# A quarter of a depthwise convolution's taps: from VectorE to ScalarE, summed by adding transfers

## The chip, the cores and the metric

The kernel runs on one core of a Trainium2 chip. Time is the device time of one execution in microseconds. The engines of a core work side by side, each through its own list of instructions in order: TensorE (PE, matrix products), VectorE (DVE), ScalarE (ACT), GpSimd (POOL) and SyncE (SP, which here only starts transfers). An instruction can wait on semaphores that other engines or transfers raise; everything behind it on its engine waits with it. A transfer is started by an instruction of SP, ACT or POOL and runs by itself afterwards.

## The reference

A two-layer trunk over 256 latent tokens and 256 context tokens of width 1024. In each layer one input projection feeds a convolution branch and an attention branch. The part that matters here is the convolution branch:

```python
def conv_branch(p_glu, dw, dw_b, ln_g, ln_b, w_o):
    a, g = jnp.split(p_glu, 2, axis=-1)
    u = a * jax.nn.sigmoid(g)
    u = dwconv1d(u, dw, dw_b)                 # depthwise, 31 taps, 512 channels
    u = jax.nn.silu(layernorm(u, ln_g, ln_b))
    return u @ w_o
```

Each of 512 channels is convolved with its own 31 weights. With channels on partitions that is 4 groups of 128 channels (j = 0 to 3) and 31 taps (t) each: 124 products of a shifted 128x256 tile with one weight per channel, summed by group. The second layer computes its output for the latent tokens alone.

## The kernel before

All matrices are float32. A product is made of three matrix products of rounded parts (L197 to L199): weight high part by input high part, weight high part by input low part, weight low part by input high part. So each unit of weights (128x1024, 512 KB) is loaded by SP into one of four `raw` buffers, rounded by ACT to `whi` (L167), and the rest `wlo` is taken by DVE (L168). For some units, listed in `ADDED`, the low part is made otherwise (`wadded`): ACT writes minus the high part into `wlo` (L217), and a transfer that POOL starts adds `raw` to it (L218). In the second layer these are three units: the query of head pair 1, the query of head pair 2, and gate 2.

The second layer's work on PE goes in this order: GLU groups 0, 1 and 2 (each gives one tile `u` of the convolution's input), the four V units in two halves (L736; ACT copies the first half's sums at L724, the second half's at L721), query 0 and key 0, GLU group 3, gate 0, query 1, key 1, and so on with attention between, then gates, the two branch products, the output product and the feed-forward part. After the first V half is copied, SP starts 16 small transfers that gather windows of V (`VW`, L728); the next weight loads stand behind these in SP's list.

The convolution is `tap` (L665 to L673): tap 0 writes `cb[j]` with the bias, each later tap is one DVE instruction that multiplies and adds into `cb[j]`. The taps of a group are put in a list when its `u` is written (L693). A generator takes three of them at each slot between matrix products; `layer_norm` takes the rest and then sums the four `cb` tiles, on POOL for the first two sums (L949, L950). `conv_tap` holds a tap back until the newest score operation of attention has been issued.

The program is written in one sequence; a scheduling layer then sorts each engine's instructions by its own estimate of when each can run, keeps the data dependences by semaphores, and gives out the buffers of a rotating pool in that order. So the place of an instruction in an engine's list is not read off the source.

Of the kernel before, what the change touches and what calls it, by code (L numbers as in the profile page):

```python
# [8 lines left out]
F32 = mybir.dt.float32  # L9
F32R = mybir.dt.float32r  # L10
BF16 = mybir.dt.bfloat16
AF = mybir.ActivationFunctionType
ALU = mybir.AluOpType
AX = mybir.AxisListType

P = 128
# [3 lines left out]
S = 256  # L20
# [5 lines left out]
TAPS = 31  # L26
# [15 lines left out]
BADA, N1G, DW, DWB, LNG, LNB, N2G, FDW, FDB, NPAR = 0, 48, 56, 180, 184, 188, 192, 200, 332, 376  # L42
# [11 lines left out]
def trunk(ctx: ExitStack, tc: tile.TileContext, xt, cvec, crow, wall, wada, params, bias_t, rope_t, out):  # L54
    nc = tc.nc
    pe, act, dve, pool, sp = nc.tensor, nc.scalar, nc.vector, nc.gpsimd, nc.sync
# [11 lines left out]
    def nm(s):  # L68
        uid[0] += 1
        return f"{s}_{uid[0]}"  # L70
# [3 lines left out]
    def psum(tag="main"):  # L74
        return psp.tile([P, 512], F32, tag=tag, bufs=BANKS[tag], name=nm(tag))

    def tmp(w=512):
        return tp.tile([P, w], F32, tag="t", bufs=5, name=nm("t"))
# [39 lines left out]
    par = cp.tile([P, DEPTH * NPAR + KD], F32, name="par")  # L118
# [27 lines left out]
    def pr(l, off, n):  # L146
        return par[:, l * NPAR + off : l * NPAR + off + n]
# [211 lines left out]
    def sum_squares(n, T, apart=False):  # L359

        at = tp.tile([P, 512], F32, tag="ss", name=nm("ss"))
        return [SumSq(T, at[:, i * T : (i + 1) * T], apart) for i in range(n)]
# [246 lines left out]
    for k in range(KD):  # L609
        if k % 2 == 0:  # L610
            sp.dma_start(x2[k // 2].rearrange("p i t -> p (i t)"), xt[k // 2])
        q = tp.tile([P, 512], F32, tag="ss", name=nm("ss")) if k == KD - 2 else tmp()
# [19 lines left out]
    for l in range(DEPTH):  # L632
        last = l == DEPTH - 1
# [4 lines left out]
        with ExitStack() if last else start as e1a:  # L638
            ea = e1a.enter_context(tc.tile_pool(name=f"ea{l}", bufs=1)) if last else ea0
# [4 lines left out]
            NU_ = KC  # L644
            us = [ea.tile([P, NS, S + 2 * PAD], F32, name=f"u{l}_{i}") for i in range(NU_)]
# [12 lines left out]
            after = [None]  # L658

            def conv_tap(j, t):  # L660
                if after[0] is not None:
                    with tc.issue_after(after[0].ins):
                        tap(j, t)
                else:
                    tap(j, t)  # L665

            def tap(j, t):
                w = par[:, l * NPAR + DW + j * TAPS + t : l * NPAR + DW + j * TAPS + t + 1]
                src = us[j % NU_][:, :, t : t + S]
                if t == 0:  # L670
                    dve.tensor_scalar(cb[j], src, w, pr(l, DWB + j, 1), ALU.mult, ALU.add)
                else:
                    dve.scalar_tensor_tensor(cb[j], src, w, cb[j], ALU.mult, ALU.add)  # L673

            rate = [0.0]

# [248 lines left out]
            with ExitStack() as e1c:  # L925
# [12 lines left out]
                def layer_norm():  # L938

                    while taps:  # L940
                        for _ in range(6 if last else 5):
                            if taps:
                                conv_tap(*taps.pop(0))
                        yield
                    pace[0] = 1.0 if last else 1.2
                    flat = [c.rearrange("p s t -> p (s t)") for c in cb]
                    sm = tp.tile([P, 512], F32, tag="ss", name=nm("ss"))
                    eng = pool if last else dve
                    eng.tensor_tensor(sm[:, :T], flat[0], flat[1], ALU.add)  # L949
                    eng.tensor_tensor(sm[:, :T], sm[:, :T], flat[2], ALU.add)  # L950
                    dve.tensor_tensor(sm[:, :T], sm[:, :T], flat[3], ALU.add)
                    for _ in range(1 if last else 5):
                        yield
                    pm = psum("po")
                    pe.matmul(pm[:, :T], one.to_broadcast([P, P]), sm[:, :T], start=True, stop=True)
                    (s2,) = sum_squares(1, T)
                    for j in range(KC):
                        dve.scalar_tensor_tensor(flat[j], pm[:, :T], -1.0 / CONV, flat[j], ALU.mult, ALU.add)
                        s2.add(flat[j], j == KC - 1)
                    for _ in range(2 if last else 5):  # L960
                        yield
                    pb = yield from rstd(s2, CONV, "po", 0 if last else 2)
                    for j in range(KC):
                        sg = tmp()
                        g, b = pr(l, LNG + j, 1), pr(l, LNB + j, 1)
                        dve.scalar_tensor_tensor(flat[j], flat[j], g, pb[:, :T], ALU.mult, ALU.mult)
                        act.activation(sg[:, :T], flat[j], AF.Silu, bias=b)
                        act.copy(sh_[j], sg[:, :T])
                        dve.tensor_tensor(sl_[j], sg[:, :T], sh_[j].bitcast(F32), ALU.subtract)
                        yield  # L970
                    if last:
                        pace[0] = 0.4
# [23 lines left out]
                for n, pc in branch(U_CO, sh_, sl_):  # L996
                    t = tmp()[:, :T]
# [59 lines left out]
        with ExitStack() as e2:  # L1057
# [96 lines left out]
            for i in range(2, KF):  # L1154
                w = [unit8(l, ups[2 * i + t]) for t in range(2)]
# [14 lines left out]
            for streams, ns in [((0, 1), range(NB)), *(((s,), range(NB, KD)) for s in range(NS))]:  # L1170
                wu = None
                c = slice(streams[0] * S, (streams[-1] + 1) * S)
                for n in ns:
                    ps = psum()
                    for k in range(KF):
                        t = n * KF + k
# [166 lines left out]
```

## Time and profile before

| | |
|---|---|
| median of three runs | 1063.33 us (1061.96 to 1065.06) |
| profiled execution, its own time | 1063.1 us |
| its span on the core | 1061.3 us |
| PE busy | 1033.7 us (97%) |
| DVE busy | 893.3 us (84%) |
| ACT busy | 567.4 us (53%) |
| POOL busy | 43.6 us (4%) |
| convolution taps on DVE, both layers (L673) | 240 instructions, 144.4 us |

The second layer's convolution runs from 695 us (first tap) to 820 us (last tap) of the span. Times in the text are microseconds from the start of the span. In a timeline row the first number is the start, the second the busy time of the merged instructions; what stands in brackets is the idle time of the engine before them and what ended it.

### The profile page before, as it was taken

Reading aid. Unit: us, or ns where it says so; the run is one execution under the profiler, and the core shown is the slowest. Engines: PE = TensorE matmul, PEld = TensorE weight load, DVE = VectorE, ACT = ScalarE, POOL = GpSimd, SP = SyncE. Lnnn points to the kernel's source line nnn. Section 1 sums busy time; section 2 is a strip of 40 time slices with the busy share of each in tenths; the row PEclk is TensorE's granted clock in tenths of the full one; section 3 lists DMA queues with packets and bytes.
Section 4 is the critical chain, followed back from the end, with each engine's and each line's share of the span. In section 5 each row is a group of like instructions: output and inputs, shape, how many; then the busy total and the mean of one; then the engine's idle time right before and its main releaser. Section 6 shows DMA issues by size and latency. Waiting matters only on the chain.

```text
span 1061.3 us, 18038 instructions
## 1 busy us (share of the span) xinstructions
PE 1033.7 (97%) x6886; PEld 932.5 (88%) x6886; DVE 893.3 (84%) x1630; ACT 567.4 (53%) x943; POOL 43.6 (4%) x59
## 2 busy tenths in 40 slices
PE   8999999999999999999989999999999999999997
PEld 6787788888879988888878889999889999999997
DVE  5568898988998798898888547899899988988883
ACT  4458767545334544443433223545776666767652
POOL 1111110011000000000000000000000000000000
PEclk9999999999999999999999999999999999999998
DMA  9988665889943344564556657666734484666781
GB/s 373 304 227 229 150 153 138 260 247 245 290 149 118 101 159 160 165 190 142 186 186 218 210 189 233 208 210 196 216 117 144 159 283 155 199 205 193 230 286 61
DMA packets 59510, 209.26 MB, mean 197 GB/s; under 512 B 7200, under 2 KB 7456, under 8 KB 59424
## 3 DMA queue, kind: packets, MB, share of 16 engines
q1 hardware_dynamic: 54384, 190.77, 54.5%
q0 software_dynamic: 4752, 17.30, 8.5%
q8 instruction: 54, 0.88, 0.3%
q14 instruction: 32, 0.26, 0.1%
q10 hardware_dynamic: 288, 0.04, 0.0%
HBM read 187.63 MB, written 1.05 MB: 178 GB/s over the span
## 4 chain that ended last, share of the span: by engine, by line
PE 39%; issue 34%; DVE 16%; ACT 5%; DMA 4%; SPq 1%; POOL 0%; DVEq 0%; ACTq 0%; POOLq 0%
PE main L197 10%; PE main L198 10%; PE main L199 10%; PE main L736 4%; DVE cb L673 4%; DMA raw<-in_wall 3%; DVE wlo L168 3%; DVE t L304 2%; SPq L728 1%; ACT whi L167 1%; PE po L230 1%; DMA own<-in_wada 1%; DVE t L403 1%; DVE h L1001 1%; DVE t L999 1%
## 5 line engine op out<-in xcount | busy, mean ns | idle before, releaser
L199 PE MATMUL main<-h,wlo 128*128 128x256 f32 (+1 forms) x1328 | 430.7, 325 | 6.6 <-DVE wlo L168 6.6
L197 PE MATMUL main<-h,whi 128*128 128x256 f32 (+1 forms) x1328 | 433.5, 327 | 1.8 <-DVE qk L882 1.2
L198 PE MATMUL main<-h,whi 128*128 128x256 f32 (+1 forms) x1328 | 430.9, 325 | 1.6 <-DVE h L1001 1.4
L167 ACT CAST whi<-raw 128x1024 fp32r<-128x1024 f32 (+1 forms) x211 | 217.6, 1036 | 230.9 <-DMA raw<-in_wall 143.9
L168 DVE TENSOR_TENSOR wlo<-raw,whi 128x1024 fp32r<-128x1024 f32 (+1 forms) x211 | 252.5, 1205 | 71.7 <-ACT whi L167 70.7
L199 PEld LDWEIGHTS main<-h,wlo 128*128 128x128 f32 x1328 | 252.8, 191 | 24.9 <-DVE wlo L168 8.0
L197 PEld LDWEIGHTS main<-h,whi 128*128 128x128 f32 x1328 | 253.2, 191 | 22.9 <-issue 1.5
L198 PEld LDWEIGHTS main<-h,whi 128*128 128x128 f32 x1328 | 253.0, 191 | 19.6 <-DVE h L1001 2.1
L673 DVE SCALAR_TENSOR_TENSOR cb<-u,par,cb 128x512 f32<-128x512 f32 (+1 forms) x240 | 144.4, 617 | 2.8
L199 PE MATMUL main<-fh,wlo 128*128 128x256 f32 (+1 forms) x386 | 119.4, 309 | 0.0
L198 PE MATMUL main<-fl,whi 128*128 128x256 f32 (+1 forms) x386 | 119.3, 309 | 0.0
L197 PE MATMUL main<-fh,whi 128*128 128x256 f32 (+1 forms) x386 | 119.3, 309 | 0.0
L304 DVE CUSTOM_DVE_ANT_0 t<-raw,sb,par 128x1024 bf16<-128x1024 f32 x72 | 91.5, 1278 | 0.5 <-ACT sb L284 0.3
L199 PEld LDWEIGHTS main<-fh,wlo 128*128 128x128 f32 x386 | 73.7, 191 | 3.8 <-DVE wlo L168 0.4
L198 PEld LDWEIGHTS main<-fl,whi 128*128 128x128 f32 x386 | 73.7, 191 | 3.4
L197 PEld LDWEIGHTS main<-fh,whi 128*128 128x128 f32 x386 | 73.7, 191 | 3.4
L304 DVE CUSTOM_DVE_ANT_0 t<-own,sb,par 128x1024 bf16<-128x1024 f32 x48 | 60.4, 1279 | 2.2 <-DMA own<-in_wada 2.2
L216 ACT CAST whi<-raw 128x1024 fp32r<-128x1024 f32 x33 | 34.6, 1047 | 40.3 <-PE main L198 34.2
L1070 ACT ACTIVATE t<-main,par 128x512 f32<-128x512 f32 (+1 forms) x82 | 50.6, 666 | 5.4 <-PE main L199 5.4
L1071 DVE SCALAR_TENSOR_TENSOR t<-main,par,t 128x510 f32<-128x510 f32 (+1 forms) x82 | 47.4, 613 | 1.3 <-ACT t L1070 1.0
L1074 DVE SCALAR_TENSOR_TENSOR t<-main,par,t 128x510 f32<-128x510 f32 (+1 forms) x82 | 46.7, 611 | 0.0
L404 ACT ACTIVATE h<-t,mod 128x256 fp32r<-128x256 f32 x56 | 25.2, 501 | 33.8 <-DVE t L403 33.6
(216 smaller groups left out, 1254.7 us busy)
## 6 DMA issues: line engine op xcount, KB each, us to landing
raw<-in_wall SPq DMA_DIRECT2D x240, 512.0 KB, 4.4
raw<-in_wada SPq DMA_DIRECT2D x64, 512.0 KB, 4.4
wlo<-raw POOLq DMA_DIRECT2D x33, 512.0 KB, 5.6
own<-in_wada SPq DMA_DIRECT2D x24, 512.0 KB, 6.2
bias<-in_bias_t SPq DMA_DIRECT2D x8, 520.0 KB, 5.1
row<-in_wada SPq DMA_DIRECT2D x8, 512.0 KB, 4.8
sb<-in_crow SPq DMA_DIRECT2D x5, 512.0 KB, 4.8
x<-in_xt SPq DMA_DIRECT2D x4, 512.0 KB, 5.1
```

Source lines behind the costliest of these rows:

```text
L167: act.copy(hi[:, c], r[:, c])
L168: dve.tensor_tensor(lo[:, c], r[:, c], hi[:, c].bitcast(F32), ALU.subtract)
L197: pe.matmul(ps, w[0], order(xh), start=start, stop=False)
L198: pe.matmul(ps, w[0], order(xl), start=False, stop=False)
L199: pe.matmul(ps, w[1], order(xh), start=False, stop=stop)
L216: act.copy(hi, r)
L304: dve.tensor_tensor_reduce(tmp().bitcast(BF16), r, v, 1.0, pr(l, BADA + n, 1), ALU.mult, ALU.add, mods[l][:, n, s : s + 1])
L673: dve.scalar_tensor_tensor(cb[j], src, w, cb[j], ALU.mult, ALU.add)
L736: mm = pe.matmul(pv[t], h1[n == 1][k][:, c], runs(w[n == 2][:, b]), start=k + n == 0, stop=k == KD - 1 and n == 2)
L1070: act.activation(c, pv_, AF.Identity, bias=pr(l, FDB + t, 1), scale=w[1])
L1071: dve.scalar_tensor_tensor(c[:, :, 1:], pv_[:, :, : S - 1], w[0], c[:, :, 1:], ALU.mult, ALU.add)
L1074: dve.scalar_tensor_tensor(c[:, :, : S - 1], pv_[:, :, 1:], w[2], c[:, :, : S - 1], ALU.mult, ALU.add)
```

## The change

In the second layer, taps 3, 7, 11, 15, 19, 23 and 27 of each group no longer go to DVE. ACT multiplies the shifted input by the weight. The first such product of a group is written into a new tile `far[j]`; each of the other six goes into one of six rotating buffers `farq`, and a transfer started by POOL adds it to `far[j]`. Before the sums of `layer_norm`, four DVE instructions add `far[j]` to `cb[j]`. So 28 DVE instructions become 28 on ACT, 24 transfers from POOL's list and 4 DVE additions. These taps no longer wait for the newest score operation.

```diff
             def conv_tap(j, t):
-                if after[0] is not None:
+                if last and t % 4 == 3 and t < TAPS - 1:
+                    far_tap(j, t)
+                elif after[0] is not None:
                     with tc.issue_after(after[0].ins):
                         tap(j, t)
                 else:
...
+            far = {}
+
+            def far_tap(j, t):
+                w = par[:, l * NPAR + DW + j * TAPS + t : l * NPAR + DW + j * TAPS + t + 1]
+                src = us[j % NU_][:, 0, t : t + S]
+                if j not in far:
+                    far[j] = ea.tile([P, S], F32, name=f"far{l}_{j}")
+                    act.activation(far[j], src, AF.Identity, scale=w)
+                else:
+                    q = ea.tile([P, S], F32, tag="farq", bufs=6, name=nm("farq"))
+                    act.activation(q, src, AF.Identity, scale=w)
+                    pool.dma_start(far[j], q, accum_op=ALU.add)
...
                     flat = [c.rearrange("p s t -> p (s t)") for c in cb]
+                    for j in far:
+                        dve.tensor_tensor(flat[j], flat[j], far[j], ALU.add)
                     sm = tp.tile([P, 512], F32, tag="ss", name=nm("ss"))
```

The change also moves instructions. ACT's list in the second layer, from the fourth V unit's rounding (`whi_6847`) to the two copies of the first V half (L724) and the rounding of query 0's weights, reads before:

```order
L167 CAST whi_6847<-raw_6846 128x1024
L691 ACTIVATE t_6825<-main_6783 128x256
L404 ACTIVATE h_5523<-t_6866,mod_106 128x256
L404 ACTIVATE h_5524<-t_6870,mod_106 128x256
L724 COPY t_6922<-main_6852 128x512
L724 COPY t_6932<-main_6853 128x512
L167 CAST whi_7009<-raw_7008 128x1024
```

The same place with the change, where the copies have line 739 (L687 is a far tap into a rotating buffer, L684 a group's first one; `h_5523` and `h_5524` are the last two input tiles of the context tokens):

```order
L687 ACTIVATE farq_7410<-u_1_6579,par 128x256
L684 ACTIVATE far_2_7484<-u_2_6580,par 128x256
L404 ACTIVATE h_5523<-t_6867,mod_106 128x256
L687 ACTIVATE farq_7627<-u_2_6580,par 128x256
L404 ACTIVATE h_5524<-t_6871,mod_106 128x256
L687 ACTIVATE farq_7667<-u_2_6580,par 128x256
L687 ACTIVATE farq_7703<-u_2_6580,par 128x256
L687 ACTIVATE farq_7861<-u_2_6580,par 128x256
L687 ACTIVATE farq_7900<-u_2_6580,par 128x256
L687 ACTIVATE farq_7939<-u_2_6580,par 128x256
L739 COPY t_6929<-main_6853 128x512
L739 COPY t_6939<-main_6854 128x512
```

All 21 far taps of groups 0, 1 and 2 now stand ahead of the V copies; 18 of them need a rotating buffer, and there are six.

POOL's list at this place held only the three adding transfers of weights. With the change it begins like this (`far_0`, `far_1`, `far_2` are the accumulators of groups 0 to 2):

```order
L688 DMA far_0_6822<-farq_6876 128x256
L688 DMA far_0_6822<-farq_6894 128x256
L688 DMA far_0_6822<-farq_6924 128x256
L688 DMA far_1_7085<-farq_7102 128x256
L688 DMA far_0_6822<-farq_6964 128x256
L688 DMA far_1_7085<-farq_7183 128x256
L688 DMA far_0_6822<-farq_6982 128x256
L688 DMA far_1_7085<-farq_7223 128x256
L688 DMA far_0_6822<-farq_7012 128x256
L688 DMA far_1_7085<-farq_7264 128x256
L688 DMA far_2_7484<-farq_7627 128x256
L688 DMA far_1_7085<-farq_7312 128x256
```

Six more such transfers follow before the first weight transfer, and group 3's stand among the second and third:

```order
L688 DMA far_2_7484<-farq_7939 128x256
L218 DMA wlo_7234<-raw_7231 128x1024
L688 DMA far_3_8143<-farq_8181 128x256
L218 DMA wlo_7421<-raw_7418 128x1024
L688 DMA far_3_8143<-farq_8268 128x256
L688 DMA far_3_8143<-farq_8367 128x256
L688 DMA far_3_8143<-farq_8373 128x256
L218 DMA wlo_7599<-raw_7596 128x1024
```

Two transfers that add to the same accumulator follow each other strictly: the later one waits, on POOL, for the earlier one's landing. The n-th far tap with a rotating buffer waits, on ACT, for the landing of the transfer that stands at place n - 6 of this list. SP's list has the same order as before.

## The prediction

> **What bounds the kernel now.** I read the busy times first, then the stretches of the second layer's convolution, then the timelines of ACT, SP, POOL and PE there.
>
> ```profile
> span 1061.3 us, 18038 instructions
> PE 1033.7 (97%) x6886; PEld 932.5 (88%) x6886; DVE 893.3 (84%) x1630; ACT 567.4 (53%) x943; POOL 43.6 (4%) x59
> 700.00:720.00 20.00, 20.00 (x111) 17.96 (x110) 20.00 (x45) 8.86 (x15) 0.00 (x0) 1.00 0.45 149
> 720.00:740.00 20.00, 20.00 (x140) 18.82 (x139) 19.96 (x44) 10.18 (x15) 0.92 (x1) 1.00 0.71 214
> 740.00:760.00 20.00, 20.00 (x154) 17.89 (x153) 16.35 (x47) 14.83 (x26) 2.46 (x3) 1.00 0.80 232
> 760.00:780.00 20.00, 19.37 (x163) 16.55 (x163) 19.93 (x52) 13.72 (x30) 0.00 (x0) 1.00 0.44 140
> 780.00:800.00 20.00, 19.36 (x196) 18.30 (x196) 19.41 (x50) 15.53 (x38) 1.58 (x1) 1.00 0.47 156
> 800.00:820.00 20.00, 19.88 (x214) 18.78 (x213) 19.32 (x37) 12.83 (x24) 0.00 (x0) 1.00 0.39 118
> 820.00:840.00 20.00, 19.03 (x169) 18.77 (x168) 18.46 (x44) 14.31 (x30) 0.71 (x1) 1.00 0.53 173
> 840.00:860.00 20.00, 19.11 (x170) 18.87 (x169) 18.51 (x37) 11.17 (x20) 0.00 (x0) 1.00 0.60 209
> ```
>
> The columns after the stretch and its length are PE, PE's weight load, DVE, ACT, POOL, granted clock, DMA share. DVE is full where the taps run, but PE hardly waits for it: PE is without work for none of the 60 us from 700 to 760 and for 0.63 + 0.64 + 0.12 + 0.97 + 0.89 = 3.25 us from 760 to 860. PE is the bound, so relief of DVE can return about 3.25 us at most, and whatever makes PE wait costs in full. ACT has room (9 to 15 of 20 us).
>
> **The change part by part: engine time.** The tap on DVE, and the nearest row for the same product on ACT (256 columns, one operand per partition):
>
> ```profile
> L673 DVE SCALAR_TENSOR_TENSOR cb<-u,par,cb 128x256 f32<-128x256 f32 x120 | 55.5, 484 | 1.3
> L861 DVE TENSOR_TENSOR t<-t,rope 128x256 f32<-128x256 f32 x8 | 3.4, 422 | 0.1
> L404 ACT ACTIVATE h<-t,mod 128x256 fp32r<-128x256 f32 x8 | 3.5, 499 | 4.2 <-DVE t L403 4.2
> ```
>
> DVE loses 28 x 55.5/120 = 13.0 us and gains four additions at 0.42, 1.7 us: 11.3 us less. ACT gains 28 x 0.5 = 14 us at most, which its idle time covers in sum. What this returns on PE (call it G) lies between 0 and 3.25 us. I take 2.8, near the upper end, because the DVE time freed is more than three times the PE idle time. Removing `issue_after` from these taps and the four additions cost nothing by themselves: the additions are in the 11.3, and the accumulators are complete some 50 us before the last taps.
>
> **The added transfers.** Nothing in the trace adds 128 KB; its nearest rows are POOL's adding transfers of 512 KB and the small gathers of V.
>
> ```profile
> q0 software_dynamic: 4752, 17.30, 8.5%
> L218 POOL DMA_DIRECT2D wlo<-raw x33: 852/862/1058, 45.6 to 750.8; - x33
> DMA to landing us min/median/max: 4.4/5.6/10.9
> wlo<-raw POOLq DMA_DIRECT2D x3, 512.0 KB, 5.7
> VW<-t SPq DMA_DIRECT2D x16, 64.0 KB, 2.1
> 733.33 1.06 ACT L217 ACTIVATE wlo<-whi 128x1024 fp32r<-128x1024 f32 x1
> 734.80 0.92 POOL L218 DMA_DIRECT2D wlo<-raw  x1 [41.07 <-DVE cb L673]
> ```
>
> POOL's queue was busy for 8.5% of 16 engines over the span with 33 transfers: 0.085 x 1061.3 / 33 = 2.73 us of moving each. A quarter of the bytes saves three quarters of that, 2.05 us: from the least landing 4.4 it leaves 2.35, from the median 5.6 it leaves 3.55. Before each transfer POOL also takes the step from the releaser's end (733.33 + 1.06 = 734.39) to the start at 734.80, 0.41 us. So the period P of a chain in which each transfer waits for the one before is 2.35 + 0.41 = 2.76 us with free queues and 3.96 us at the median. The ends are 2.1 + 0.41 = 2.51 (the V gathers, half the bytes, no addition) and 5.6 + 0.41 = 6.0 (if the bytes did not matter). The excess of the median over the least, 1.2 us, is what other traffic costs; this layer's three ran with 1.3 at DMA shares of 0.71 and 0.80. The chain runs mostly in the stretch of share 0.45, so I take 1.2 x 0.45 / 0.76 = 0.7 and P = 3.46.
>
> **Where the chain holds ACT.** ACT's far taps wait for a rotating buffer, and behind them stand the copies of V, then SP's gathers, then the weight loads:
>
> ```profile
> 695.01 0.41 DVE L693 SCALAR_TENSOR_TENSOR u<-t,sc 128x256 f32<-128x256 f32 x1
> 713.53 1.24 ACT L724 COPY t<-main 128x512 f32<-128x512 f32 x2 [3.91 <-PE main L736]
> 714.15 10.94 SPq L728 DMA_DIRECT2D VW<-t  x16
> 725.19 0.53 SPq L164 DMA_DIRECT2D raw<-in_wall  x1
> 725.81 0.40 SPq L154 DMA_DIRECT2D raw<-in_wall  x1
> raw<-in_wall SPq DMA_DIRECT2D x240, 512.0 KB, 4.4
> 731.95 0.42 ACT L881 ACTIVATE qk<-t 128x256 fp32r<-128x256 f32 x1 [1.74 <-DVE t L864]
> 732.27 1.03 ACT L216 CAST whi<-raw 128x1024 fp32r<-128x1024 f32 x1
> 740.29 0.28 PE L198 MATMUL main<-h,whi 128*128 128x256 f32 x1
> 740.52 0.38 PE L199 MATMUL main<-h,wlo 128*128 128x256 f32 x1
> ```
>
> Group 0's input is written at 695.42. `far_0` (0.5), a rounding that stands between (1.06) and the first `farq` (0.5) end at 697.4 or so, and POOL starts transfer 1 at about 697.7. The 18th `farq` on ACT needs the landing of transfer 12 in POOL's list. Transfers 1, 2, 3 are a chain in group 0; transfer 4 (group 1) is issued 0.87 behind 3; 6, 8, 10 and 12 each follow the one before by P. So 12 starts at 697.7 + 6P + 0.87 and lands P - 0.41 later: 698.2 + 7P. One more far tap, and the copies of V start at about 698.6 + 7P instead of 713.53. They are late by D = 7P - 14.9 = 9.3 us.
>
> SP's 16 gathers start with these copies (714.15 is 0.62 behind 713.53) and take 11 us of SP's list; behind them are gate 0's load (725.19) and query 1's (725.81). Before, query 1's weights land at 725.81 + 4.4 = 730.2, and ACT comes to them at 732.27, because it is held until 731.95 by the rotary part of query 0: 2.1 us of slack. The rest has none. ACT writes `wlo`, POOL's transfer is issued at 734.80 and lands 5.7 later, at 740.5, and PE's first use of it starts at 740.52, where 0.11 us after 740.29 would be its pace. So PE waits there for S = D - 2.1 = 7P - 17.0 = 7.2 us. The waits on the way (query 0's rounding behind the late copies, gate 0's late load) lie inside these 7.2, since they come from the same lateness. `h_5524`, needed at the end of the second V half (723.6), stands behind transfer 7's landing, about 697.7 + 5P - 0.4 = 714.6: covered.
>
> POOL's own list is later still, but does not decide: transfer 18 starts at about 697.7 + 10P + 1.8, so query 1's could be issued from 700.8 + 10P = 735.4, while its input is ready only at 734.8 + 7.2 = 742.0. It decides from 700.8 + 10P > 717.8 + 7P, P over 5.7. Gate 2's transfer stands behind four of group 3:
>
> ```profile
> 742.60 0.41 DVE L693 SCALAR_TENSOR_TENSOR u<-t,main 128x256 f32<-128x256 f32 x1
> 750.78 0.86 POOL L218 DMA_DIRECT2D wlo<-raw  x1 [6.95 <-ACT qk L881]
> ```
>
> Counted from group 3's input, 743.0, the first starts about 1.8 later and the fourth 3P behind it, so gate 2's goes out at about 744.8 + 10.4 + 1.3 = 756.5, 5.7 late, when everything is 7.2 late. Covered.
>
> **Sum.** S - G = 7.2 - 2.8 = 4.4 us. The profiled execution took 1063.1 us (span 1061.3 and 1.8 around it), 0.2 under the median of the three runs: 1063.1 + 4.4 = 1067.5 us.
>
> **The rivals.**
>
> *The chain is short enough (not slower).* If the queues are free when the far transfers arrive, P is 2.76, S is 2.3 and the net is 2.3 - 2.8 = -0.5: 1062.6 us. For it: the share of 0.45 in 700 to 720 means idle queues half of the time, and late copies also delay the loads that compete. Against it: the median landing of 33 transfers is 1.2 above the least. It decides below P = 3.1, where the net is +1.9.
>
> The Trainium skill, page "DMA: Bandwidth & Descriptors", section "Anatomy of one DMA — SWDGE (gpsimd) path", gives about 2.0 us fixed plus bytes over 436 GB/s for such a transfer, 2.3 us for 128 KB; as an estimate from it P would be 2.71, S 2.0 and the time 1062.3. The same rule makes 3.2 us of 512 KB, where the trace has 4.4 at least and 5.6 at the median, so it runs low here, and I keep to the rows.
>
> *Faster.* If the landings come so soon that ACT is never held (S = 0 from P = 2.43 down), only the relief of DVE is left: up to 3.25 us, 1059.9 us. For it: DVE full in five of the stretches quoted. Against it: even the V gathers with half the bytes give P = 2.51.
>
> *The transfers collide with the weight loads.* At the landing of this layer's own three, 5.7, P is 5.7 - 2.05 + 0.41 = 4.06, S is 11.4 and the time 1063.1 + 11.4 - 2.8 = 1071.7; each further 0.1 us of P adds 0.7. For it: these three ran beside the loads that come next in SP's list, and the first links fall among the V units' loads. Against it: loads stop when ACT does. It decides above P = 3.9.
>
> **How the numbers follow.** Forecast (P 3.1 to 3.9, 1065 to 1070.6): 0.54. Short chain: 0.27. Collision: 0.14. Faster: 0.05. About 0.3%, 3.2 us, is what this kernel's timing can tell from no change, so slower means over 1066.5, P over 3.3: 0.42 of the forecast's 0.54 and the collision's 0.14, 0.56. Faster means under 1060.1: 0.05. The rest, 0.39, is no difference to be told. The range runs from 1061.5 (P 2.6 with this G) to 1074 (P 4.4); the forecast's own is 1065 to 1070.6.
>
> **What would show it.** In the changed profile: the period of far transfers on POOL (3.1 to 3.9 us, 24 issues of 0.87); ACT idle before far taps, released by transfers, 1 to 2 us at a time between 703 and 722; the V copies at 720 to 724 instead of 713.5; SP's gathers right behind; PE waiting some 5 to 9 us in total between 724 and 750, most of it for query 1's `wlo` from POOL; PE idle from 760 to 860 down by 2 to 3 us. I am wrong if the V copies stay before 718, if PE's wait sits elsewhere (at the end of the convolution, or at gate 2), or if the idle time after 760 does not shrink.

## The result: slower by 1.3%, and more than forecast

The changed kernel takes 1076.09 us (median of 6 runs, 1073.0 to 1080.78) against 1063.18 us before (1060.83 to 1065.06): a ratio of 1.0127, 95% interval 1.01 to 1.0154. The forecast was 1067.5 with a range up to 1074. The profiled execution took 1075.25 us.

The busy times of the changed kernel in the stretches of the second layer's convolution, in the columns of the prediction's table (PE, PE's weight load, DVE, ACT, POOL, granted clock, DMA share, GB/s):

```profile
700.00:720.00 20.00, 20.00 (x103) 17.72 (x102) 12.14 (x26) 9.71 (x21) 7.40 (x9) 1.00 0.67 165
720.00:740.00 20.00, 14.18 (x67) 12.60 (x66) 17.85 (x40) 7.24 (x11) 7.41 (x9) 0.83 0.67 135
740.00:760.00 20.00, 16.00 (x112) 15.27 (x112) 10.84 (x22) 13.52 (x22) 3.45 (x4) 0.91 0.96 279
780.00:800.00 20.00, 17.73 (x146) 15.52 (x145) 19.59 (x54) 15.78 (x37) 0.00 (x0) 0.91 0.49 162
```

PE, which had no idle time from 700 to 760, now misses 5.8 and 4.0 us there, and its granted clock is below 1.00 in three of these stretches. The waits of PE from 690 to 900, summed by what ended them (us in total, times, longest):

```profile
PE main L197 <- ACT whi L167: 5.4, 1, 5.4
PE main L199 <- DMA wlo<-raw: 4.0, 1, 4.0
PE pt L495 <- ACT pT L564: 1.8, 1, 1.8
```

The first is the wait for query 0's rounded weights, the second the wait for query 1's low part. ACT's timeline shows where the lateness begins:

```profile
708.94 0.51 ACT L687 ACTIVATE farq<-u,par 128x256 f32<-128x256 f32 x1 [3.57 <-DMA far<-farq]
...
725.41 0.51 ACT L687 ACTIVATE farq<-u,par 128x256 f32<-128x256 f32 x1 [1.64 <-DMA far<-farq]
725.83 1.05 ACT L739 COPY t<-main 128x512 f32<-128x512 f32 x2
726.77 2.94 ACT L167 CAST whi<-raw 128x1024 fp32r<-128x1024 f32 x3
...
742.58 1.07 ACT L216 CAST whi<-raw 128x1024 fp32r<-128x1024 f32 x1 [0.20 <-DMA raw<-in_wall]
```

In brackets stands how long ACT waited for a far transfer to land, in the last row for a load. The sum of these waits is in ACT's own table of waits from 700 to 745, and the input of group 0 (here line 708) in DVE's table of that tile:

```profile
ACT farq L687 <- DMA far<-farq: 14.7, 10, 3.6
```

```profile
L708 DVE SCALAR_TENSOR_TENSOR u<-t,sc x1: 411/411/411, 693.7 to 693.7; 128x256 f32<-128x256 f32 x1
```

Group 0's input is written at 693.7 here and was written at 695.01 before: this execution is 1.3 us ahead when the change sets in. The V copies come at 725.83 instead of 713.53, so they are 12.3 + 1.3 = 13.6 us late. SP's gathers start right behind them, and the weight loads behind the gathers:

```profile
726.42 10.04 SPq L743 DMA_DIRECT2D VW<-t  x16
...
737.18 0.41 SPq L154 DMA_DIRECT2D raw<-in_wall  x1
```

Query 1's load goes out at 737.18 (before: 725.81); ACT rounds it at 742.58, POOL adds the rest, and PE gets it at 751.68 (before: 740.52). That is 11.2 + 1.3 = 12.5 us late, about as much as this execution lost in all (1075.25 - 1063.1 = 12.2); what PE loses and makes up behind it is added up further down. POOL's timeline and the landings of its transfers:

```profile
696.40 0.92 POOL L688 DMA_DIRECT2D far<-farq  x1 [4.36 <-ACT farq L687]
700.49 0.87 POOL L688 DMA_DIRECT2D far<-farq  x1 [3.17 <-ACT far L684]
703.81 1.77 POOL L688 DMA_DIRECT2D far<-farq  x2 [2.44 <-ACT farq L687]
...
711.31 0.86 POOL L688 DMA_DIRECT2D far<-farq  x1 [1.13 <-ACT farq L687]
...
714.63 0.89 POOL L688 DMA_DIRECT2D far<-farq  x1 [0.35 <-ACT farq L687]
...
719.60 1.75 POOL L688 DMA_DIRECT2D far<-farq  x2 [2.25 <-ACT farq L687]
722.69 0.88 POOL L688 DMA_DIRECT2D far<-farq  x1 [1.35 <-DMA far<-farq]
...
745.14 0.87 POOL L218 DMA_DIRECT2D wlo<-raw  x1 [6.17 <-ACT qk L896]
```

```profile
far<-farq POOLq DMA_DIRECT2D x24, 128.0 KB, 3.0
```

The rows show the transfers on the prediction's path: 1, 2, 3 and 4 (the last two merged at 703.81; transfer 4 starts at 704.35), then 6, 8, 10 and 12. Its links, start to start, are 4.09 and 3.32, then 6.96 from transfer 4 to 6, and 3.32, 4.97 and 3.09. Twelve transfers, seven links, lie between the first start at 696.40 and the landing that lets ACT go on at 725.41: by the prediction's formula (the landing comes at the first start + 7P + 0.5) that is P = (725.4 - 696.4 - 0.5) / 7 = 4.07 us, where 3.46 was forecast.

### The profile page after: what moved, and what is told of

The parts are those of the page before. It is cut to its first block, busy times and chain, and to the rows that moved or that the text cites. A ratio compares the mean times of both kernels' runs of the same rounds, so it can differ in the third digit from the quotient of the medians.

```text
span 1073.5 us, 18099 instructions
## 1 busy us (share of the span) xinstructions
PE 1040.0 (97%) x6886; PEld 939.3 (87%) x6886; DVE 883.7 (82%) x1606; ACT 579.7 (54%) x971; POOL 64.4 (6%) x83
## 4 chain that ended last, share of the span: by engine, by line
PE 55%; DVE 21%; DMA 10%; ACT 8%; issue 4%; SPq 1%; DVEq 0%; ACTq 0%; POOL 0%; POOLq 0%
PE main L197 16%; PE main L199 16%; PE main L198 16%; DMA raw<-in_wall 7%; DVE wlo L168 4%; DVE t L304 4%; DVE cb L675 4%; PE main L751 2%; DMA far<-farq 2%; ACT whi L167 2%; DVE t L1088 1%; DVE t L1091 1%; SPq L743 1%; PE sc L197 1%; PE sc L199 1%
## 5 line engine op out<-in xcount | busy, mean ns | idle before, releaser
L199 PEld LDWEIGHTS main<-h,wlo 128*128 128x128 f32 x1328 | 255.4, 193 | 28.4 <-DVE wlo L168 7.2
L197 PEld LDWEIGHTS main<-h,whi 128*128 128x128 f32 x1328 | 256.2, 193 | 27.5 <-ACT whi L167 5.9
L198 PEld LDWEIGHTS main<-h,whi 128*128 128x128 f32 x1328 | 255.8, 193 | 18.4 <-DVE h L1018 0.9
L675 DVE SCALAR_TENSOR_TENSOR cb<-u,par,cb 128x512 f32<-128x512 f32 (+1 forms) x212 | 130.8, 631 | 2.6
L1113 ACT CAST fh<-t 128x256 fp32r<-128x256 f32 (+1 forms) x43 | 21.9, 509 | 37.2 <-DVE t L1103 37.2
```

The lines of the kernel that those rows point to most:

```text
L197: pe.matmul(ps, w[0], order(xh), start=start, stop=False)
L198: pe.matmul(ps, w[0], order(xl), start=False, stop=False)
L199: pe.matmul(ps, w[1], order(xh), start=False, stop=stop)
L1113: lastev[0] = act.copy(a, ca_)
```

## The experiments

Two theories were open. One: two holds, ACT's wait for a rotating buffer (hold 1) and POOL's list, in which query 1's low part stands behind 18 far transfers (hold 2), both made by the chain of landings. The other: the transfers' traffic, or ACT's 14 us of products, slow the weights as such. Beside these, the size of the relief G had to be measured, and the half clock of PE, of which the prediction does not speak.

Executions differ by some microseconds before the convolution begins, so places in time are compared by their distance from group 0's input (`u`), for the V copies 18.5 us in the kernel before (713.53 - 695.01).

| kernel | us, median | ratio to before, 95% |
|---|---|---|
| the change | 1076.09 | 1.0127 (1.01 to 1.0154) |
| E1 sixteen buffers | 1078.34 | 1.0133 (1.0097 to 1.0169) |
| E2 28 taps left out | 1064.8 | 1.0009 (0.999 to 1.0028) |
| E3 transfers without ACT's products | 1076.93 | 1.014 (1.0115 to 1.0166) |
| E4 the change, PE's first wait filled | 1077.22 | 1.0147 (1.0115 to 1.018) |
| E5 low parts on DVE, six buffers | 1075.86 | 1.0123 (1.0101 to 1.0145) |
| E6 low parts on DVE, sixteen buffers | 1063.53 | 1.0017 (1.0001 to 1.0032) |
| E7 additions by POOL itself | 1072.13 | 1.0094 (1.0079 to 1.0109) |
| E8 far taps spread behind the V copies | 1075.34 | 1.0121 (1.0105 to 1.0138) |
| E9 low parts on DVE, ten buffers | 1067.56 | 1.0054 (1.0034 to 1.0074) |
| E10 as E5, PE's wait filled | 1075.21 | 1.0116 (1.0095 to 1.0137) |
| E11 E5 again | 1074.92 | 1.0125 (1.0103 to 1.0147) |
| E12 two accumulators a group | 1070.31 | 1.0072 (1.0055 to 1.009) |

### E1, sixteen buffers: the first hold away

```diff
-                    q = ea.tile([P, S], F32, tag="farq", bufs=6, name=nm("farq"))
+                    q = ea.tile([P, S], F32, tag="farq", bufs=16, name=nm("farq"))
```

> The changed kernel with sixteen rotating buffers instead of six, so that ACT's far taps of groups 0 to 2 need no transfer to have landed. Theory (ACT is held by waits for landings, which makes the V copies late): ACT's idle time before far taps falls from 14.7 us to under 2; V copies at 714 to 717 instead of 725.8; the 5.4 us wait of PE before query 0 is gone. What is left is POOL's list, where query 1's low part stands behind 18 far transfers: at the 4.07 us that a link took in the changed kernel its transfer is issued at 697.7 + 10 x 4.07 + 1.8 + 0.9 = 741 and PE waits up to 7 us for it, at 3.3 us nothing. Time 1061 to 1070. Rival 1 (the far transfers' traffic slows the weight loads): traffic is the same or denser, PE still waits before query 0, time about 1076. Rival 2 (the 14 us of extra products on ACT make it late by themselves): V copies stay after 720, time about 1076.

1078.34 us: no gain. But the first hold is gone. The V copies start at 718.95 in an execution whose group 0 came at 700.9, so 18.1 us behind it, as before (713.53 - 695.01 = 18.5), and ACT does not wait for a far transfer at all. PE has one wait from 700 to 760, and POOL's timeline shows why:

```profile
PE main L199 <- DMA wlo<-raw: 9.0, 1, 9.0
```

```profile
731.38 0.87 POOL L688 DMA_DIRECT2D far<-farq  x1 [2.02 <-DMA far<-farq]
...
740.04 0.86 POOL L688 DMA_DIRECT2D far<-farq  x1 [6.10 <-DMA far<-farq]
...
749.44 0.86 POOL L688 DMA_DIRECT2D far<-farq  x1 [2.60 <-ACT farq L687]
750.07 1.13 POOL L218 DMA_DIRECT2D wlo<-raw  x1
```

Query 1's low part is issued directly behind the 18th far transfer, at 750.07, and that one had to wait for its predecessors one by one. Hold 2 has taken the place of hold 1, at about the same price. The wait of 9.0 is above the 7 that were allowed for it, and the time above 1070: late links fall among the weight loads, which now run. The transfer started at 731.38 (group 1) is followed by the next of its group only at 740.04, 8.7 us later.

### E2, the 28 taps left out

```diff
-                    far_tap(j, t)
+                    pass
...
-                    for j in far:
-                        dve.tensor_tensor(flat[j], flat[j], far[j], ALU.add)
```

> The 28 taps are left out of the computation altogether: no product on ACT, no transfer, no addition. It measures the relief of DVE by itself, with 28 taps fewer instead of 28 taps for 4 additions. Theory: 1063.2 - 2.9 = 1060.3 us, PE's idle time from 760 to 860 down from 3.25 us to under 0.5, no half-clock stretch after 700. Rival (the recovery of 2.9 us at the end of the changed kernel is only work that was waiting anyway, relief is 0): 1063.2 us, idle time stays at 3.

1064.8 us, ratio 1.0009: the kernel as a whole gains nothing that can be measured; the interval allows a gain of 1.1 us at most, not the 2.9 of the expectation. PE's waits from 760 to 860, first of the kernel before, then of this one:

```profile
PE main L197 <- DVE qk L882: 1.2, 2, 0.6
PE pt L370 <- DVE ss L356: 1.0, 1, 1.0
PE main L199 <- DVE wlo L168: 0.9, 1, 0.9
```

```profile
PE pt L495 <- ACT pT L564: 1.8, 1, 1.8
PE main L199 <- DVE wlo L168: 0.9, 1, 0.9
PE main L197 <- DVE qk L897: 0.2, 1, 0.2
```

3.1 us before and 2.9 now. Waits for DVE do shrink, from 3.1 to 1.1, but PE then waits 1.8 for ACT's copy of the attention weights. That wait has a cause of its own, in the order of ACT's list. Two of the four copies and the step on the next key or query (`qk<-main`), first in the kernel before, then here:

```profile
777.21 0.49 ACT L564 COPY pT<-pt 128x384 f32<-128x384 f32 x1
777.58 0.50 ACT L564 COPY pT<-main 128x384 f32<-128x384 f32 x1
780.10 0.38 ACT L881 ACTIVATE qk<-main 128x256 fp32r<-128x256 f32 x1 [2.03 <-DVE t L860]
```

```profile
777.63 0.38 ACT L896 ACTIVATE qk<-main 128x256 fp32r<-128x256 f32 x1 [1.98 <-DVE t L875]
777.91 0.47 ACT L564 COPY pT<-pt 128x384 f32<-128x384 f32 x1
```

In both kernels ACT waits 2.0 us for DVE at that step. Before, the copies stand ahead of it; here they stand behind it, and PE's next scores wait for them. Compare PE's place, that is the start of the same product in both traces: this execution is 0.7 us ahead of the kernel before at 760, 1.3 ahead at the transposes whose results are copied (773.45 against 774.73), 0.6 behind after them (778.44 against 777.83) and 1.6 ahead at the end of the span (1059.7 against 1061.3). So 0.6 + 2.2 = 2.8 us were returned, as forecast, and 1.9 were lost at the copies. E2 does not measure the relief by itself, since leaving out the taps also changed the order of ACT's list. The same order and a wait of 1.8 to 2.0 us stand in the changed kernel and in E1, E4 to E7 and E9 to E12; the kernel before, E3 and E8 have the copies first. No run has the taps left out and the old order. The trace is of one of the fastest of ten executions (1061.44 us; the slowest took 1068.81); what the slower ones lose is not on record.

### E3, the transfers without ACT's products: traffic and POOL's list

```diff
-                elif after[0] is not None:
+                if after[0] is not None:
...
-                    q = ea.tile([P, S], F32, tag="farq", bufs=6, name=nm("farq"))
-                    act.activation(q, src, AF.Identity, scale=w)
-                    pool.dma_start(far[j], q, accum_op=ALU.add)
+                    pool.dma_start(far[j], src, accum_op=ALU.add)
...
-                    for j in far:
-                        dve.tensor_tensor(flat[j], flat[j], far[j], ALU.add)
```

> All 124 taps stay on DVE as in the kernel before. The 24 adding transfers of 128 KB are still started by POOL, four accumulators, same chains, but they add the shifted input itself and the result is not used: ACT makes only the first product of each group and has no rotating buffer to wait for. Theory: the V copies are at 713 to 715 and PE does not wait before query 0; traffic alone costs under 2 us there; POOL's list still holds query 1's low part back as in the kernel with sixteen buffers. Time 1063 to 1072, all of it at query 1's low part. Rival 1 (traffic slows the weight loads): PE waits for rounded weights from 727 on, at several places, and the time is near 1076 + 2.9 = 1079, since the relief is missing.

1076.93 us, with ACT and DVE as before and the V copies on time (713.20). PE's only wait from 700 to 760 is again the one for query 1's low part, 7.7 us; there is none before query 0 and none for another unit's rounded weights. So the place is the theory's and not that of the traffic; the time is 5 us over the theory's upper end, and against the rival's 1079 it alone would not decide. E6 does.

### E5 and E6, the low parts on DVE: the second hold away, and both

```diff
-ADDED = {*((0, U_IN + i) for i in (*range(19), 20, 22, 24, 26, 28)), *((0, u) for u in (U_NA + 1, U_NA + 3, *range(U_CO, U_CO + 4))), *((1, U_IN + i) for i in (7, 8, 16))}
+ADDED = {*((0, U_IN + i) for i in (*range(19), 20, 22, 24, 26, 28)), *((0, u) for u in (U_NA + 1, U_NA + 3, *range(U_CO, U_CO + 4)))}
```

E6 also has `bufs=16`. With these, the lists of PE and SP stay as in the changed kernel.

> The changed kernel with six buffers, but the low parts of query 1, query 2 and gate 2 are made by DVE, as for the other units, so no weight stands behind the far transfers in POOL's list; far transfers and their traffic stay. Theory (two separate holds, ACT's wait for a buffer and POOL's list, of which the later one sets PE's wait): the first hold is left, V copies at 724 to 727, PE waits 5 to 6 us before query 0 and runs 6.8 us at half clock behind it, the wait at query 1's low part (4.0) is gone: 1063.2 + 5.4 + 3.4 = 1072 us. Rival (traffic of the far transfers slows every weight load, wherever the low part is made): PE waits near query 1 as before, 1076 us.

> The same with sixteen buffers: both holds are gone and only the traffic, the 14 us of products on ACT and the relief of DVE are left. Theory (two holds): no wait of PE over 1 us between 700 and 760, V copies at 713 to 716, time 1062 to 1065 us, the same as the kernel before. Rival (traffic): waits for rounded weights of 3 us or more between 724 and 760, 1068 us or more. Rival (ACT's own products): V copies after 718.

E5: 1075.86 us; E6: 1063.53 us. With the first hold alone the loss is whole, although the wait at query 1's low part is gone: 5.7 us before query 0, half clock behind it, and later waits for ACT. The expected 1072 was too low; taking the second hold away returns nothing while the first stands. With both away the loss is gone. E6 carries the same 24 far transfers and the same products on ACT, and PE waits for nothing from 690 to 760:

```profile
700.00:720.00 20.00, 20.00 (x108) 17.88 (x107) 19.96 (x44) 14.30 (x30) 8.47 (x10) 1.00 0.83 208
720.00:740.00 20.00, 20.00 (x143) 18.90 (x142) 18.92 (x38) 9.66 (x14) 4.61 (x6) 1.00 0.99 281
```

```profile
far<-farq POOLq DMA_DIRECT2D x24, 128.0 KB, 4.0
```

The transfer engines are busier than in the changed kernel (0.83 and 0.99 against 0.67 and 0.67), and a far transfer takes longer (median 4.0 us against 3.0). It costs nothing, since nobody stands behind it. This excludes traffic and ACT's products as causes of the loss before 760. It is also the best that was measured with the change: 0.01% to 0.32% above the kernel before. Its trace has the wait for ACT's copies, as in E2, 1.9 us long and with half clock from 778.8 to 782.2 behind it. What the three low parts on DVE cost or bring by themselves, no run measures.

Together: hold 1 alone 1075.86, hold 2 alone 1078.34 (or 1076.93 in E3), both 1076.09, none 1063.53. The holds do not add up; the later of the two sets how late PE is with queries 0 and 1.

### E9, ten buffers: how much hold for how many buffers

> The kernel with the three low parts on DVE, with ten rotating buffers, between the six (1075.9 us) and the sixteen (1063.5 us) that were run. Theory (ACT is held by the landing of an older transfer, here the 8th in POOL's list where with six buffers it was the 12th): by the prediction's own chain the 8th starts two links earlier, so the V copies come at 698.6 + 5 x 4.07 = 719 instead of 727, PE's wait before query 0 falls from 5.7 us to 0 to 1 and the time to 1064 to 1067 us. Rival (the number of buffers matters only through the whole queue of 18, no chain): 1070 us or more.

1067.56 us, between six and sixteen, and 0.6 above the expected range. The V copies start at 717.36 with group 0's input at 693.5, 23.9 us behind it, against 18.5 before: 5.3 us late. By the chain they should be 719 - 713.5 = 5.5 late. ACT waits 6.9 us in all for far transfers; with six buffers it was 14.7. PE's wait at query 0 is down to 1.3 us, there for a low part from DVE.

### E4, E10 and E11, the waiting time of PE filled: what the half clock costs

PE's timeline in the changed kernel, at its two waits:

```profile
727.88 0.58 PE L197 MATMUL main<-h,whi 128*128 128x256 f32 x1 [5.36 <-ACT whi L167]
...
731.01 0.42 PE L198 MATMUL main<-h,whi 128*128 128x256 f32 x1
731.22 0.42 PE L199 MATMUL main<-h,wlo 128*128 128x256 f32 x1
...
747.29 0.28 PE L197 MATMUL main<-h,whi 128*128 128x256 f32 x1
747.40 0.28 PE L198 MATMUL main<-h,whi 128*128 128x256 f32 x1
751.68 0.58 PE L199 MATMUL main<-h,wlo 128*128 128x256 f32 x1 [4.00 <-DMA wlo<-raw]
```

Behind a wait a product takes 0.42 us and starts every 0.21; elsewhere 0.28 and every 0.11. The stretches at a clock of 0.50 last from 727.3 to 734.1 and from 751.2 to 754.6, and a third one from 792.2 to 795.6: 13.6 us, at half speed 6.8 us of work lost. The first is followed by the wait for query 1's low part, where PE would have waited longer had it come sooner; the other two are followed by no such wait. The Trainium skill, page "TensorE: Matmul & The Clock Gate", section "Part 1: The HAM clock gate (the "warmup" mystery)", says that the clock falls to half after an idle window of about 3.4 us and comes back after as long a busy one. The trace agrees in the lengths, 6.8, 3.4 and 3.4 us, but not in what goes before: the third stretch follows a wait of only 1.8 us (for ACT's copies, until 791.64), and the same wait in E2 is followed by no such stretch. E10 fills the wait of E5 with products into a bank of their own, as the diff shows; E4 does the same in the changed kernel, but writes into `ps` itself:

```diff
-                return group(psum(tag), unit8(l, U_IN + t), *h1, c)
+                w, ps = unit8(l, U_IN + t), psum(tag)
+                if last and t == T_Q:
+                    fill, x = psum("pt"), h1[0][7]
+                    for i in range(48):
+                        pe.matmul(fill[:, c], x[:, 0:P], runs(x[:, c]), start=True, stop=True)
+                return group(ps, w, *h1, c)
```

> The changed kernel with 48 products added on PE ahead of query 0, into the sums that query 0's first product overwrites: they fill the 5.4 us in which PE waits there and change nothing else. Theory (a wait of PE is followed by a stretch at half clock): the half-clock stretch 727.3 to 734.1 is gone, 3.4 us are saved there, time 1072.7 us. Rival (the records of a half clock are no loss of their own, the time goes by when weights arrive): the same 1076.

> The kernel with six buffers and the three low parts on DVE, with 48 products of no use added on PE ahead of query 0, into a bank that nothing else uses then: they fill the 5.7 us in which PE waits there. One rounding of weights (gate 0) also comes one place earlier in ACT's list. Theory (the half-clock stretch of 6.8 us behind the wait costs 3.4 us of its own, and here no second hold hides it): the stretch is gone, 1075.9 - 3.4 = 1072.5 us. Rival (what follows is set by ACT and by weights, the half clock is hidden): no change, 1075.9 us.

> The kernel with six buffers and the three low parts on DVE once more, beside the one whose wait is filled, so that both are timed on the same chip: 1075.9 us (first hold, alone), PE's wait of 5.7 us before query 0 and the half-clock stretch behind it.

E4: 1077.22 us. E10: 1075.21 us, with E11 beside it at 1074.92. The stretch from 720 to 740 in E10, and what SP does there:

```profile
720.00:740.00 20.00, 20.00 (x129) 18.52 (x128) 19.23 (x41) 8.82 (x15) 7.84 (x9) 1.00 0.65 117
```

```profile
728.03 10.04 SPq L748 DMA_DIRECT2D VW<-t  x16
738.17 1.03 SPq L164 DMA_DIRECT2D raw<-in_wall  x2
```

The half clock is gone from this stretch (1.00), and the 3.4 us of the expectation did not come; the rival is the nearer one. The executions of E10 lie from 1071.89 to 1077.72 and those of E11 from 1073.52 to 1077.86, so a gain of 1 or 2 us could hide among them. E11 itself did not come out as expected: its trace has a wait of 4.1 us before query 0, not 5.7, and 3.4 us of half clock behind it, not 6.8, so that the stretch was worth 1.7 us there. The next weights start to be loaded at 738.17, because the gathers stand ahead of them, and up to 760 PE waits 1.1 us more for DVE and 0.3 for a low part. E4 says less than E10, since its fill had to wait 1.5 us for a bank.

### E7, the additions computed by POOL

```diff
-                    pool.dma_start(far[j], q, accum_op=ALU.add)
+                    pool.tensor_tensor(far[j], far[j], q, ALU.add)
```

> The changed kernel with the 24 adding transfers replaced by 24 additions that POOL computes itself, in the same place of its list; ACT's products and six buffers stay. Theory (what costs is the landing of each transfer, 4.07 us a link, not the number of instructions): POOL needs 0.7 to 1.6 us for an addition (its two sums of the same shape took 0.73 and 1.58 us), so buffers come free before ACT needs them, V copies at 713 to 718, query 1's low part not late; time 1062 to 1065 us. Rival (ACT's own 14 us): V copies after 718, 1067 us or more. Rival (POOL's additions slow the taps on DVE): taps over 0.52 us each instead of 0.46, and PE waits for DVE from 760 on, 1066 us.

1072.13 us. The theory's part holds: the V copies start at 715.93, 18.8 us behind group 0's input (697.1), on time. The rival that was given third is what happened, at a higher price than its 1066. DVE's instructions from 697 to 725, first of E7, then of E6, whose additions are transfers (count, busy us, mean ns):

```profile
L675 DVE SCALAR_TENSOR_TENSOR cb<-u,par,cb 128x256 f32<-128x256 f32 x22 | 12.5, 624 | 0.1
```

```profile
L675 DVE SCALAR_TENSOR_TENSOR cb<-u,par,cb 128x256 f32<-128x256 f32 x32 | 13.2, 484 | 0.0
```

A tap takes 0.62 us instead of 0.48 beside POOL's additions. DVE, which was full, falls behind with the rotary part of query 0; ACT waits 6.5 us for it, rounds query 1 late, and PE waits 3.8 us for query 1's low part. The Trainium skill, page "SBUF — State Buffer", section "SBUF: two separate sides", says that a DVE instruction with two inputs in that memory and a GpSimd instruction that reads it take turns at a common port, each holding it to its end. The longer taps (0.62 against 0.48 us) agree with that.

### E8, the far taps spread behind the V copies

```diff
+                taken = range(3, TAPS - 1, 4) if last else ()
+                taps.extend((j, t) for t in range(TAPS) if t not in taken)
+                hold.extend((j, t) for t in taken)
...
+                    if hold and gone:
+                        hold.sort(key=lambda a: (a[1], a[0]))
...
+                            with tc.issue_after(lastcast[0].ins):
+                                far_tap(*hold.pop(0))
```

`hold` keeps the far taps, and `gone` is filled once the V copies are written down in the program. The edit, shown here in part, also puts POOL's two sums behind its transfers.

> The change's work in another order: ACT's far taps stand behind the copies of V and are spread over the list, the three groups in turn, three taps in two slots, so that a buffer is asked for about as often as one comes free; the same 24 adding transfers, six buffers. Theory: V copies at 713.5, no wait of PE before query 0; query 1's low part stands behind 11 far transfers in three chains, which are started from about 715 on at 1.4 to 2 us each, so it goes out at about 737 to 742 against 734.8: wait at query 1 of 2 to 6 us, half clock behind it, 1065 to 1071 us. Rival (traffic): waits at several units, 1073 us or more.

1075.34 us. The V copies are on time (712.81 with group 0's input at 695.0), PE does not wait before query 0, and query 1's low part goes out at 735.28, nearly in time (PE waits 1.6 us for it). The loss comes one unit later:

```profile
749.10 0.88 POOL L688 DMA_DIRECT2D far<-farq  x1 [1.92 <-DMA far<-farq]
753.95 0.87 POOL L688 DMA_DIRECT2D far<-farq  x1 [3.98 <-DMA far<-farq]
754.65 1.06 POOL L220 DMA_DIRECT2D wlo<-raw  x1
```

Query 2's low part (line 220 here) goes out only behind two links of group 3 in POOL's list, and PE waits 5.8 us for it. It is the second hold again, at another unit than expected and 4 us dearer than the range given.

### E12, two accumulators for each group

```diff
+                j = (j, t // 4 % 2)
...
-                        dve.tensor_tensor(flat[j], flat[j], far[j], ALU.add)
+                        dve.tensor_tensor(flat[j[0]], flat[j[0]], far[j], ALU.add)
```

> The changed kernel with two accumulators for each group, taken in turn: 20 transfers in eight chains of 2 or 3 links instead of 24 in four chains of 6; 8 first products and 8 additions on DVE instead of 4; six buffers, low parts as in the changed kernel. Theory (both holds come from the length of the chain of landings): transfers go in pairs, so the 9th, for whose buffer the last far tap before the V copies waits, lands at about 697.7 + 4 x 4.07 + 1.8 = 716; V copies at 715 to 718, query 1's low part no longer behind late transfers (15 ahead of it, the last started before 735): 1062 to 1066 us. Rival (each transfer takes its time in POOL's queue whatever it adds to): 1072 us or more.

1070.31 us: about half of the loss is gone, less than expected, and less bad than the rival. The V copies come at 721.63 with group 0's input at 696.0, 25.6 us behind it and 7.1 late, where 1.5 to 4.5 were expected. The first links show why:

```profile
699.12 1.82 POOL L689 DMA_DIRECT2D far<-farq  x2 [4.83 <-ACT farq L688]
705.13 0.86 POOL L689 DMA_DIRECT2D far<-farq  x1 [4.18 <-DMA far<-farq]
```

The first link takes 6.0 us, not 4.07, with two transfers under way. The pair that the changed kernel started at 719.60 and 720.13, when SP started no load, was followed by the next of its chain at 722.69, 3.1 us after the first. So a pair alone does not make a link long. Weight loads alone do: in the changed kernel a far transfer that had no other adding transfer beside it landed in 2.9 us with no load under way (started at 730.96) and in 7.8 with four (774.77). The traces of the change, E1, E3 to E6 and E8 to E12 together say the same: without another adding transfer beside it, a far transfer landed in 2.9 us at the median with at most one load under way (33 transfers) and in 5.4 with three or more (21). The first pair of E12 had two loads beside it as well; how much of its 6.0 us is the pair stays open.

## Why the prediction was wrong, step by step

**The mechanism** was right: buffers that a chain of landings frees, ACT held before them, the V copies, the gathers and the loads behind the copies, PE waiting at query 1's low part. E6 and E9 show it. **Its two formulas** hold. The V copies at 698.6 + 7P give, with the measured P of 4.07, 727.1; they came at 725.8 in an execution 1.3 ahead. Since this P was worked out from the landing just before the copies, that is no test of the chain; E9 is one (5.3 us late, 5.5 by the chain). S = 7P - 17.0 gives 11.5; PE got query 1's low part 12.5 late, of which 0.8 is that transfer's own landing (751.68 - 745.14 = 6.5 instead of 5.7).

**The first step that failed is P = 3.46.** Each 0.1 us counts seven times, so 0.61 us of P are 4.3 us of the result. P was added up from a landing with free queues (2.35), a step to the next start (0.41) and traffic (0.7), and all three were too low. The least landing of the 24 far transfers is 2.7 us: "A quarter of the bytes saves three quarters of that, 2.05 us" came out as 1.7 (4.4 - 2.7). That makes about 2.2 us over seven links. From a landing to the next start it took 0.63 to 0.65 us on five of the path's six steps and 0.39 on one: 1.1 us more. The traffic, from "I take 1.2 x 0.45 / 0.76 = 0.7", came to 6.2 us over the path instead of 4.9: 1.3 us more, and it was not spread as a mean share of 20 us would have it. More than half of it, 3.7 us, is in transfer 4 (6.3 us to its landing), which starts beside three weight loads that SP begins at 704.12. (Transfer 4 started 0.54 us behind transfer 3 and not 0.87, which takes 0.3 off.) The collision rival named that place and priced P at 4.06; it was given 0.14. That a landing is longer where loads are under way shows in the counts under E12.

**The second is G = 2.8.** The time was given back, and taken again at a place that the prediction put at nothing: the order of ACT's list further on. By PE's place the changed kernel is 1.9 us ahead at the end of the V units (722.14 against 724.07), 11.2 behind at query 1's low part (751.68 against 740.52), 12.6 behind after the half clock there (754.74 against 742.18), 11.9 at the transposes ahead of ACT's copies (786.67 against 774.73), 15.3 after the wait for them and the half clock behind it (795.63 against 780.28), and 12.2 at the end of the span. So 0.6 + 3.1 = 3.7 us were made up and 3.4 lost at the copies; G is 0.3 net. That all of the 3.7 is relief of DVE is not shown; E2, which has neither far taps nor transfers, makes up 2.8 in the same stretch.

**The sum.** From the V units to 754.74 PE loses 12.6 + 1.9 = 14.5 us, where S was 7.2. Of the 7.3 us more, 4.3 are P, 0.8 the landing of query 1's transfer, 1.4 the half clock behind it; 0.8 are not accounted for. G is 2.5 short. The lead of 1.9 us that this execution had before the change sets in has nothing to do with the forecast and takes off as much: 7.3 + 2.5 - 1.9 = 7.9, beside the 7.75 by which the profiled execution missed the forecast.

**The waits "on the way lie inside these 7.2":** right in that they come from one lateness, wrong in what would be seen. The greater part (5.4) is before query 0, the smaller (4.0) at query 1. The half clock was not foreseen. Its first stretch lies inside, since PE waits 4.0 us behind it; the second and the third put PE further back (the second by 1.4 us).

**"POOL's own list ... does not decide":** right for the changed kernel, where its transfer at 745.14 waits for ACT and not for the list. But E1 shows how close it stands: with the first hold gone it costs as much. The sentence compared the list with an input that was itself late by S. **Gate 2 covered:** right, PE has no wait there.

**Of the signs named**, the period (4.07, not 3.1 to 3.9), the V copies (725.8, not 720 to 724) and the drop of PE's idle time after 760 by 2 to 3 us missed; 24 issues of 0.87, ACT released by transfers, SP's gathers right behind and PE's wait of 5 to 9 us (9.9) came as said or close to it.

## What to carry to other kernels

A buffer that a transfer frees puts the whole in-order list of its engine behind that transfer: count the buffers against the products queued up, and ask what stands next in the list. Where the time runs through two lists, taking one hold away shows nothing until the other is gone; only the four combinations (E1, E5, E6 and the change) told that. And leaving the work out once shows what moving it can bring, but read the lists of the other engines with it: here the relief came, and a new order of two of ACT's instructions took most of it.

## What was not expected of the hardware

The half clock behind PE's waits: products every 0.21 us instead of 0.11, for 3.4 or 6.8 us. Taking the first stretch away brought nothing that shows in E10's time; the second, which no wait follows, put PE 1.4 us further back (11.2 us late at 751.68, 12.6 at 754.74). A wait of 1.8 us was followed by half clock in the changed kernel and not in E2. A link of the chain of adding transfers took from 3.1 us (the changed kernel, from 719.60) to 8.7 us (E1, from 731.38). And DVE's taps take 0.62 us instead of 0.48 while POOL adds tiles of the same size.
